# Walking the 512 columns of the feed-forward products in another order, layer by layer

## The chip, the cores and the metric

The kernel runs on one core of one Trainium2 chip, in one launch. The time is the device time of an execution in microseconds (us). The kernel before has a median of 2347.55 us over three runs (2344.4 to 2348.18).

## What is computed

Two blocks of a transformer work on 512 tokens of 1024 features in float32, with conditioning vectors that scale, shift and gate every layer. Of the six layers four are feed-forward layers, and the change touches these alone:

```python
def swiglu(y, w_gate, w_up, w_down):          # block 1, layers 1 and 3; hidden width 2816
    return (jax.nn.silu(y @ w_gate) * (y @ w_up)) @ w_down
...
y = jnp.square(jax.nn.relu(h @ mlp_w1[i])) @ mlp_w2[i]    # block 2, both MLPs; hidden width 4096
```

The others are a mixer of an mLSTM and a gated recurrence, gated linear attention, and differential attention. Their projections use the same two product helpers as the feed-forward layers.

## The kernel before

Every float32 value that goes into a large product is cut into two parts of type fp32r, a rounded high part and the rest (`parts2`, lines 320 to 328, for weights; line 606 for hidden values). A product of 128 rows of the contraction is then three matmuls into the same PSUM columns: high by high, high by low, low by high. Each matmul loads a stationary operand of 128 x 128 (LDWEIGHTS) and streams a moving operand (`rhs`) of up to 512 columns, one PSUM bank of 512 float32 per partition being the result.

Two helpers issue these matmuls. `fm` (lines 359 to 372) makes a feature-major product: the stationary operand is 128 columns of a weight, the moving one the tokens of the layer's input `X`, either all 512 (`FULL`) or a half of 256 (`HALVES`). `tm` (lines 374 to 388) makes a token-major product: the stationary operand is 128 tokens, the moving one 512 columns of a weight unit. In both, the moving operand and the result `p` are slices whose columns lie next to each other in memory.

`ffn` (lines 580 to 645) runs a layer in parts of its hidden width, `parts` tiles of 128 at a time. For every tile `hidden` calls `fm` (twice where there is a gate and an up weight), and ScalarE and VectorE turn the two PSUM results into the two parts of the hidden value, which lie in the buffers XB or XA. Then for two halves of the output columns and four blocks of 128 tokens `tm` multiplies the part by the down weight, and ScalarE or VectorE adds the result to `y` or to the residual. In the layers after the first, the first tiles (`nsplit`: 3 in the second feed-forward layer, 6 in the MLPs) run by halves of 256 tokens, so that they can start on the first half of the input. In the last layer `last_half` (lines 522 to 547) makes the last part, and its last token block has two products of 256 columns (lines 526 to 533).

PSUM banks are handed out in turn by role (`FFN_BANKS`, line 47: six for products, two for transposes). The program is one order of instructions per engine with semaphores between them; SyncE issues the loads of raw weights, ScalarE writes the high parts and VectorE the low parts, ahead of the products that use them. Conditioning vectors of later layers are computed meanwhile on VectorE and GpSimd at a pace set by `work` (lines 280 to 285).

The four layers start at lines 745, 1212, 1378 and 1613.

Of the kernel before, what the change touches and what calls it, by code (L numbers as in the profile page):

```python
# [35 lines left out]
def kernel(ctx: ExitStack, tc: tile.TileContext, a: dict, out: bass.AP):  # L36
    nc = tc.nc
    V, S, G, PE = nc.vector, nc.scalar, nc.gpsimd, nc.tensor
# [71 lines left out]
    def act(out, in_, func, **kw):  # L110
        """an activation; those of one table stay together, in the order of the program"""
# [12 lines left out]
    # two regions that hold plain values and rounded ones in turn, as tensors over the same bytes  # L124
# [93 lines left out]
    h = const.tile([128, 4, D], F32, tag="h", name="h")  # L218
# [7 lines left out]
    def ada_steps(w, c0, sc, bias, name, post=None, f=1.0):  # L226
        """one conditioning vector in eight steps: as columns, or (bias a row) as a row on every partition, times f
        times the row post"""
# [51 lines left out]
    def work(us):  # L280
        """conditioning vectors keep pace with the products"""
        clk[0] += us
        while jobs and clk[1] + clk[2] <= clk[0]:
            clk[1] += clk[2]
            bg()
# [44 lines left out]
    def group(w, k0, kn, c0, cn, uc=128):  # L330
        """[kn*128 rows, cn columns] of w as units of uc columns, each [128, 2, kn, uc]"""
# [9 lines left out]
    def group_k(w, k0, kn, c0, cn, uk):  # L341
        """the same cut into units of uk row tiles, each [128, 2, uk, cn]"""
# [14 lines left out]
    products, due = [], [0]  # L357

    def fm(p, wt, X, span, c=0):
        """feature-major product: 128 columns of a unit against the tokens of span"""  # L360
# [3 lines left out]
        for k in range(kn):  # L364
            xh, xl = X[k]
            wh, wl = wt[:, 0, k, c:c + 128], wt[:, 1, k, c:c + 128]
            PE.matmul(p, lhsT=wh, rhs=xh[:, s:s + n], start=k == 0, stop=False)  # L367
            PE.matmul(p, lhsT=wh, rhs=xl[:, s:s + n], start=False, stop=False)  # L368
            done = PE.matmul(p, lhsT=wl, rhs=xh[:, s:s + n], start=False, stop=k == kn - 1)  # L369
# [4 lines left out]
    def tm(p, wts, X, blk, c=0):  # L374
        """token-major product: 128 tokens against the columns of the units"""
# [5 lines left out]
        for wt in wts:  # L381
            for k in range(wt.shape[2]):
                xh, xl = X[n]
                PE.matmul(p, lhsT=xh[:, s:s + 128], rhs=wt[:, 0, k, cs], start=n == 0, stop=False)  # L384
                PE.matmul(p, lhsT=xh[:, s:s + 128], rhs=wt[:, 1, k, cs], start=False, stop=False)  # L385
                done = PE.matmul(p, lhsT=xl[:, s:s + 128], rhs=wt[:, 0, k, cs], start=False, stop=n == last)  # L386
# [6 lines left out]
    class Parts(list):  # L393
        """the two parts of a layer's input, by rows of features, and the tensors that hold them"""
# [22 lines left out]
    class Sums:  # L417
        """sums of squares of two token blocks by halves of the columns, and from them 1 / rms"""
# [18 lines left out]
    def scaled_to(dst, blk, r):  # L437
        """dst = the block of h times r"""
# [7 lines left out]
    def to_X(X, y, A, sh, half, role="pt"):  # L446
        """two token blocks of y to feature-major, modulated, in parts"""
# [25 lines left out]
    class PostEnd:  # L473
        """h += row * y / rms(y), then the next layer's input"""
# [25 lines left out]
    class GateEnd:  # L500
        """h += row * y, then the next layer's input; y in two parts, the first of them to early()"""
# [20 lines left out]
    def last_half(w, k0, X, y, row, gain):  # L522
        """h += row * y, then the last normalisation and out, by token blocks and parts of their columns"""
# [27 lines left out]
    def flush(ns=()):  # L551
        """the transposes of late, in parts behind the last ns of the products"""
# [94 lines left out]
    def tm_full(w, X, c0, sink):  # L647
        """token-major product with 512 columns"""
# [8 lines left out]
    # ======== start ========  # L657
# [1002 lines left out]
```

## Time and profile before

| | us |
|---|---|
| median of three runs | 2347.55 |
| lowest and highest | 2344.4, 2348.18 |
| span of the profiled execution | 2346.7 |
| PE busy in it | 2296.0 |
| VectorE busy | 1415.6 |
| ScalarE busy | 924.5 |
| GpSimd busy | 189.9 |

The profile states no time of its own for the profiled execution beside its span, from the first to the last instruction; the median of the runs lies 0.85 us above it. The page has the busy time of each engine (PE is TensorE's matmul, PEld its weight load, which overlaps), the span in 40 slices of 58.7 us, and the chain of work that ended last. Matmuls are pipelined: the duration of one includes its fill and drain, so that two matmuls overlap in the rows, and what a matmul costs in a stream is the distance from its start to the next one's.

### The profile page before, as it was taken

Reading aid. Unit: us, or ns where it says so; the run is one execution under the profiler, and the core shown is the slowest. Engines: PE = TensorE matmul, PEld = TensorE weight load, DVE = VectorE, ACT = ScalarE, POOL = GpSimd, SP = SyncE. Lnnn points to the kernel's source line nnn. Section 1 sums busy time; section 2 is a strip of 40 time slices with the busy share of each in tenths; the row PEclk is TensorE's granted clock in tenths of the full one; section 3 lists DMA queues with packets and bytes.
Section 4 is the critical chain, followed back from the end, with each engine's and each line's share of the span. In section 5 each row is a group of like instructions: output and inputs, shape, how many; then the busy total and the mean of one; then the engine's idle time right before and its main releaser. Section 6 shows DMA issues by size and latency. Waiting matters only on the chain.

```text
span 2346.7 us, 27950 instructions
## 1 busy us (share of the span) xinstructions
PE 2296.0 (98%) x10920; PEld 1849.9 (79%) x10920; DVE 1415.6 (60%) x2371; ACT 924.5 (39%) x1722; POOL 189.9 (8%) x126
## 2 busy tenths in 40 slices
PE   6999999999999999999999999999999999999998
PEld 4788887888678888888877887888776767888887
DVE  7846455765858645455654775567755577634364
ACT  4332224643656332224644443222345456323222
POOL 0111111000001101010000011011000010100000
PEclk9999999999999999999999999999999999999999
DMA  9755444445212655451432264445341312423221
GB/s 269 233 174 176 145 162 72 109 108 101 71 54 74 214 165 176 127 164 61 130 123 90 72 197 153 140 142 167 120 129 55 113 63 70 138 90 101 88 91 62
DMA packets 211733, 292.60 MB, mean 125 GB/s; under 512 B 7121, under 2 KB 120192, under 8 KB 211600
## 3 DMA queue, kind: packets, MB, share of 16 engines
q1 hardware_dynamic: 210960, 289.74, 40.7%
q8 instruction: 86, 1.41, 0.2%
q10 hardware_dynamic: 640, 1.07, 0.1%
q14 instruction: 47, 0.39, 0.1%
HBM read 288.68 MB, written 2.10 MB: 124 GB/s over the span
## 4 chain that ended last, share of the span: by engine, by line
PE 87%; DVE 5%; ACT 3%; DMA 2%; issue 2%; POOL 1%; POOLq 0%; SPq 0%; ACTq 0%; DVEq 0%
PE PS L386 13%; PE PS L367 13%; PE PS L384 13%; PE PS L368 13%; PE PS L385 13%; PE PS L369 13%; PE PS L1466 1%; DMA araw<-in_ada_w_dram 1%; ACT RS L118 1%; DVE w L328 1%; PE PS L901 1%; POOL sm L407 1%; PE PS L1495 1%; ACT tmp L118 1%; ACT w L118 1%
## 5 line engine op out<-in xcount | busy, mean ns | idle before, releaser
L328 DVE TENSOR_TENSOR w<-raw,w 128x1024 fp32r<-128x1024 f32 (+1 forms) x392 | 472.3, 1210 | 431.1 <-ACT w L118 430.4
L118 ACT ACTIVATE w<-raw 128x1024 fp32r<-128x1024 f32 (+1 forms) x392 | 389.2, 1000 | 519.7 <-PE PS L386 292.2
L368 PE MATMUL PS<-XAr,w 128*128 128x512 f32 (+1 forms) x1328 | 492.7, 371 | 1.1 <-DVE XAr L466 0.6
L369 PE MATMUL PS<-XAr,w 128*128 128x512 f32 (+1 forms) x1328 | 491.3, 370 | 0.0
L367 PE MATMUL PS<-XAr,w 128*128 128x512 f32 (+1 forms) x1328 | 489.7, 372 | 0.1
L384 PE MATMUL PS<-w,XAr 128*128 128x512 f32 x806 | 322.1, 400 | 1.0 <-DVE XAr L465 0.8
L385 PE MATMUL PS<-w,XAr 128*128 128x512 f32 x806 | 319.4, 397 | 0.0
L386 PE MATMUL PS<-w,XAr 128*128 128x512 f32 x806 | 319.1, 397 | 0.0
L368 PEld LDWEIGHTS PS<-XAr,w 128*128 128x128 f32 x1328 | 251.5, 189 | 48.1 <-DVE XAr L690 1.1
L367 PEld LDWEIGHTS PS<-XAr,w 128*128 128x128 f32 x1328 | 250.3, 189 | 48.9 <-issue 1.6
L369 PEld LDWEIGHTS PS<-XAr,w 128*128 128x128 f32 x1328 | 251.2, 189 | 45.2
L386 PE MATMUL PS<-w,XBr 128*128 128x512 f32 x704 | 279.8, 398 | 2.4 <-DVE XBr L606 2.0
L385 PE MATMUL PS<-w,XBr 128*128 128x512 f32 x704 | 280.2, 398 | 0.0
L384 PE MATMUL PS<-w,XBr 128*128 128x512 f32 x704 | 279.1, 397 | 0.1
L118 ACT ACTIVATE tmp<-PS 128x512 f32<-128x512 f32 (+3 forms) x227 | 104.4, 465 | 429.2 <-PE PS L369 339.5
L245 DVE SCALAR_TENSOR_TENSOR acc<-araw,silu_c,acc 128x512 f32<-128x512 f32 x266 | 199.3, 749 | 69.3 <-DMA araw<-in_ada_w_dram 65.0
L253 POOL PARTITION_ALL_REDUCE tmp<-acc x38 | 132.5, 3486 | 1068.4 <-DVE acc L245 700.0
L384 PEld LDWEIGHTS PS<-w,XAr 128*128 128x128 f32 x806 | 151.9, 188 | 37.7 <-ACT tmp L118 1.6
L385 PEld LDWEIGHTS PS<-w,XAr 128*128 128x128 f32 x806 | 152.0, 189 | 36.1 <-issue 1.6
L386 PEld LDWEIGHTS PS<-w,XAr 128*128 128x128 f32 x806 | 151.9, 189 | 36.1 <-issue 0.8
L386 PEld LDWEIGHTS PS<-w,XBr 128*128 128x128 f32 x704 | 132.3, 188 | 34.4 <-DVE XBr L606 2.8
L384 PEld LDWEIGHTS PS<-w,XBr 128*128 128x128 f32 x704 | 132.3, 188 | 33.4 <-ACT RS L118 0.5
(297 smaller groups left out, 2508.4 us busy)
## 6 DMA issues: line engine op xcount, KB each, us to landing
araw<-in_ada_w_dram SPq DMA_DIRECT2D x152, 512.0 KB
raw<-in_mlp_w_dram SPq DMA_DIRECT2D x56, 1024.0 KB
raw<-in_ffn_w_gate_dram SPq DMA_DIRECT2D x20, 1024.0 KB
raw<-in_ffn_w_up_dram SPq DMA_DIRECT2D x20, 1024.0 KB
raw<-in_ffn_w_down_dram SPq DMA_DIRECT2D x20, 1024.0 KB
raw<-in_w_in_dram SPq DMA_DIRECT2D x16, 1024.0 KB
raw<-in_gla_w_in_dram SPq DMA_DIRECT2D x12, 1024.0 KB
raw<-in_diff_w_in_dram SPq DMA_DIRECT2D x12, 1024.0 KB
```

The lines of the kernel that those rows point to most:

```text
L118: ins = S.activation(out, in_, func, **kw)
L245: V.scalar_tensor_tensor(acc, raw[:, k, :], col, acc, op0=ALU.mult, op1=ALU.add)
L253: G.partition_all_reduce(red, acc, channels=128, reduce_op=bass_isa.ReduceOp.add)
L328: V.tensor_tensor(wt[:, 1, ks], src[:, ks], wt[:, 0, ks].bitcast(F32), op=ALU.subtract)
L367: PE.matmul(p, lhsT=wh, rhs=xh[:, s:s + n], start=k == 0, stop=False)
L368: PE.matmul(p, lhsT=wh, rhs=xl[:, s:s + n], start=False, stop=False)
L369: done = PE.matmul(p, lhsT=wl, rhs=xh[:, s:s + n], start=False, stop=k == kn - 1)
L384: PE.matmul(p, lhsT=xh[:, s:s + 128], rhs=wt[:, 0, k, cs], start=n == 0, stop=False)
L385: PE.matmul(p, lhsT=xh[:, s:s + 128], rhs=wt[:, 1, k, cs], start=False, stop=False)
L386: done = PE.matmul(p, lhsT=xl[:, s:s + 128], rhs=wt[:, 0, k, cs], start=False, stop=n == last)
L407: G.tensor_tensor(r, ms, mhalf[:, 0:w], op=ALU.pow)
L901: PE.matmul(p[:, c * 128:(c + 1) * 128], lhsT=L[:, c * 128:(c + 1) * 128], rhs=R[:, c * 128:(c + 1) * 128], start=True, stop=True)
```

## The change

`fm` and `tm` send the moving operand and the result of each matmul through a new helper, `walked`. Where a walk is set and the operand has 512 columns, it views them as `a` blocks of `b` runs of `c` columns and reads or writes them run by run: the first run of each block, then the second run of each block, and so on. Both operands are walked alike, so that every value lands where it did before. The stationary operand is as it was, and so are the matmuls, their number and their order. A variable, `walk`, is set ahead of each feed-forward layer and cleared after it; operands of 256 columns are left as they were.

| layer | a, c | runs of a matmul | from one run to the next |
|---|---|---|---|
| feed-forward 1 | 2, 2 | 256 of 2 columns | 256 columns on, or back |
| feed-forward 2 | 4, 16 | 32 of 16 columns | 128 columns on, or back |
| MLP 1 | 2, 8 | 64 of 8 columns | 256 columns on, or back |
| MLP 2 | 2, 64 | 8 of 64 columns | 256 columns on, or back |

```diff
+    walk = [None]
+
+    def walked(ap):
+
+        if walk[0] is None or ap.shape[1] != 512:
+            return ap
+        a_, c_ = walk[0]
+        return ap.rearrange("p (a b c) -> p b a c", a=a_, c=c_)
...
     def fm(p, wt, X, span, c=0):
...
-            PE.matmul(p, lhsT=wh, rhs=xh[:, s:s + n], start=k == 0, stop=False)
-            PE.matmul(p, lhsT=wh, rhs=xl[:, s:s + n], start=False, stop=False)
-            done = PE.matmul(p, lhsT=wl, rhs=xh[:, s:s + n], start=False, stop=k == kn - 1)
+            xh, xl = walked(xh[:, s:s + n]), walked(xl[:, s:s + n])
+            PE.matmul(walked(p), lhsT=wh, rhs=xh, start=k == 0, stop=False)
+            PE.matmul(walked(p), lhsT=wh, rhs=xl, start=False, stop=False)
+            done = PE.matmul(walked(p), lhsT=wl, rhs=xh, start=False, stop=k == kn - 1)
...
     def tm(p, wts, X, blk, c=0):
...
-                PE.matmul(p, lhsT=xh[:, s:s + 128], rhs=wt[:, 0, k, cs], start=n == 0, stop=False)
-                PE.matmul(p, lhsT=xh[:, s:s + 128], rhs=wt[:, 1, k, cs], start=False, stop=False)
-                done = PE.matmul(p, lhsT=xl[:, s:s + 128], rhs=wt[:, 0, k, cs], start=False, stop=n == last)
+                wh, wl, p_ = walked(wt[:, 0, k, cs]), walked(wt[:, 1, k, cs]), walked(p)
+                PE.matmul(p_, lhsT=xh[:, s:s + 128], rhs=wh, start=n == 0, stop=False)
+                PE.matmul(p_, lhsT=xh[:, s:s + 128], rhs=wl, start=False, stop=False)
+                done = PE.matmul(p_, lhsT=xl[:, s:s + 128], rhs=wh, start=False, stop=n == last)
...
+    walk[0] = 2, 2
     Xm = new_X("xa")
     ffn(X, a["ffn1_w_gate"][0], ...
+    walk[0] = None
...
+    walk[0] = 4, 16
     X3 = new_X("xa")
     ffn(X2, a["ffn2_w_gate"][0], ...
+    walk[0] = None
...
+    walk[0] = 2, 8
     X5 = new_X("xa")
     ffn(X4, a["mlp_w1_2"][0], None, ...
+    walk[0] = None
...
+    walk[0] = 2, 64
     ffn(X6, a["mlp_w1_2"][1], None, ...
```

The rest of the diff takes out comments and docstrings.

## Rows read from the trace of the kernel before

**Rows 1.** The page: busy time of each engine; the span in 40 slices.
```profile
PE 2296.0 (98%) x10920; PEld 1849.9 (79%) x10920; DVE 1415.6 (60%) x2371; ACT 924.5 (39%) x1722; POOL 189.9 (8%) x126
...
PE   6999999999999999999999999999999999999998
...
PEclk9999999999999999999999999999999999999999
```

**Rows 2.** The page: the chain that ended last, by engine and by line.
```profile
PE 87%; DVE 5%; ACT 3%; DMA 2%; issue 2%; POOL 1%; POOLq 0%; SPq 0%; ACTq 0%; DVEq 0%
PE PS L386 13%; PE PS L367 13%; PE PS L384 13%; PE PS L368 13%; PE PS L385 13%; PE PS L369 13%; PE PS L1466 1%; DMA araw<-in_ada_w_dram 1%; ACT RS L118 1%; DVE w L328 1%; PE PS L901 1%; POOL sm L407 1%; PE PS L1495 1%; ACT tmp L118 1%; ACT w L118 1%
```

**Rows 3.** Windows of the four feed-forward layers; the header names the columns.
```profile
core 0: us, PE busy (x) PEld busy (x) DVE busy (x) ACT busy (x) POOL busy (x), PEclk, DMA share, GB/s
55.00:410.00 355.00, 354.39 (x1526) 283.81 (x1526) 209.40 (x304) 111.49 (x158) 47.17 (x40) 1.00 0.55 162
770.00:1112.00 342.00, 341.42 (x1475) 274.25 (x1474) 189.29 (x247) 101.66 (x145) 32.99 (x13) 1.00 0.46 149
1377.00:1705.00 328.00, 326.02 (x1402) 261.48 (x1401) 214.00 (x286) 100.78 (x142) 34.42 (x10) 1.00 0.48 154
2015.00:2346.00 331.00, 324.63 (x1411) 261.95 (x1409) 153.38 (x194) 96.67 (x137) 6.27 (x5) 0.99 0.30 95
```

**Rows 4.** Timeline of PE, matmuls of `fm`: start us, duration us, line.
```profile
770.24 0.40 PE L367 MATMUL PS<-XAr,w 128*128 128x512 f32 x1
770.47 0.39 PE L368 MATMUL PS<-XAr,w 128*128 128x512 f32 x1
...
781.95 0.40 PE L369 MATMUL PS<-XAr,w 128*128 128x512 f32 x1
```

**Rows 5.** Timeline of PE, matmuls of `tm` in the first layer.
```profile
399.52 0.39 PE L384 MATMUL PS<-w,XBr 128*128 128x512 f32 x1
...
402.55 0.40 PE L385 MATMUL PS<-w,XBr 128*128 128x512 f32 x1
```

**Rows 6.** Timeline of PE, matmuls of 256 columns in the mixer.
```profile
429.53 0.28 PE L369 MATMUL PS<-XAr,w 128*128 128x256 f32 x1
...
430.59 0.28 PE L369 MATMUL PS<-XAr,w 128*128 128x256 f32 x1
```

**Rows 7.** Timeline of PE, products of plain float32, 256 columns, in block 2.
```profile
1171.03 0.60 PE L1312 MATMUL PS<-XBf,RS 128*128 128x256 f32 x2
1171.46 0.59 PE L1317 MATMUL PS<-XBf,tmp 128*128 128x256 f32 x2
1171.89 1.03 PE L1312 MATMUL PS<-XBf,RS 128*128 128x256 f32 x4
1172.75 0.59 PE L1314 MATMUL PS<-st,XBf 128*128 128x256 f32 x2
```

**Rows 8.** Lines 925 and 606 on VectorE (durations ns min/median/max).
```profile
L925 DVE TENSOR_TENSOR tmp<-XBf x24: 415/418/428, 441.7 to 599.6; 128x256 f32<-128x256 f32 x24
L606 DVE TENSOR_TENSOR XBr<-tmp,XBr x85: 412/684/2732, 65.9 to 1675.1; 128x512 fp32r<-128x512 f32 x67, 128x256 fp32r<-128x256 f32 x18
```

**Rows 9.** Groups of PE by line and shape in 55 to 410 us: count, busy us, mean ns, idle before.
```profile
L368 PE MATMUL PS<-XAr,w 128*128 128x512 f32 x325 | 128.8, 397 | 0.0
...
L386 PE MATMUL PS<-w,XBr 128*128 128x512 f32 x176 | 69.9, 397 | 0.0
```

More of the change, by code (lines that the diff above doesn't have):

```diff
@@ L393 @@
     class Parts(list):
+        pass
     def new_X(bank="xa"):
```

## The prediction

> **What bounds the kernel now.** I read the page first: PE is busy 2296.0 of 2346.7 us, 9 tenths or more in every slice but the first and the last, at full granted clock, while VectorE has 60% and ScalarE 39% [rows 1]. Busy time of a pipelined engine could still hide waits, so the chain comes next: PE has 87% of it, and the six lines of `fm` and `tm` 13% each, 78% together [rows 2]. Then the four layers that the change touches, as windows: in 55 to 410 us PE is busy 354.39 of 355.00 us, in the others 341.42 of 342, 326.02 of 328 and 324.63 of 331, at a granted clock of 1.00, 1.00, 1.00 and 0.99 [rows 3]. The groups of that first window show no idle time ahead of the product lines [rows 9]. So in these layers nothing is waited for; a matmul starts when the one before has streamed. What one costs is the distance between starts, not its duration (397 ns on average, which overlaps the next): from 770.24 to 781.95 us there are 50 steps of `fm`, 234.2 ns each [rows 4], and from 399.52 to 402.55 us 13 steps of `tm`, 233.1 ns each [rows 5].
>
> Is that time the stream's, or a fixed cost of a matmul (its weight load, its dispatch)? Matmuls of 256 columns are 9 steps in 1.06 us apart, 117.8 ns [rows 6]: half of the columns, half of the time. So the time is proportional to the columns, 0.457 ns each, and the stream itself is the bound. [...] Plain float32 products stream at 1.72 us for 8 matmuls of 256 columns, 215 ns each, 0.84 ns a column [rows 7].
>
> **What the change does to this.** It adds no instruction, no wait, no transfer, and moves none: the count of matmuls and weight loads, the semaphores, the loads of SyncE and the work of the other engines are the same, and since both views of a bank and of an operand reach from its first to its last column, what has to wait for what is the same too. The only thing that can change is the time of a column in the stream of a walked matmul. How many are walked follows from the code (512 columns, walk set):
>
> - feed-forward 1, runs of 2: 22 tiles x 2 weights x 8 rows x 3 = 1056 in `fm`, 22 x 2 x 4 x 3 = 528 in `tm`: 1584 (the first window has three lines of `fm` with some 325 and three of `tm` with 176 [rows 9]; the rest of `fm` lies before 55 us, between waits for the first data)
> - feed-forward 2, runs of 16: 19 x 2 x 8 x 3 = 912, and 528: 1440
> - MLP 1, runs of 8: 26 x 8 x 3 = 624, and 32 x 2 x 4 x 3 = 768: 1392
> - MLP 2, runs of 64: 1392 less 18 that have 256 columns: 1374
>
> In all 5790, at 234 ns some 1355 us, 58% of the span. There is no cover: PE has no idle time in these layers, so every ns on a matmul of the first layer is 1.58 us of the end, and on all 5790 it is 5.79 us.
>
> What a hop between runs costs the stream, the trace of before does not show: every matmul in it reads and writes neighbouring columns. [...] Above: the slowest stream that the trace has on this engine, 0.84 ns a column [rows 7], 430 ns a matmul, +196 ns; or, if a run of two costs as much to fetch as four neighbouring columns do now, 2 x 234 = 468 ns, +234.
>
> The nearest row for a hop is on another engine: line 925 reads and writes 256 columns in runs of 1, 2, 4, 8, 16 and 32 with as many left out between, and takes 415 to 428 ns over all 24; the fastest 256 columns of line 606, side by side, take 412 [rows 8]. That is at most 16 ns over 256 columns and no trend to six sizes of run. VectorE is slower per column than PE, so this bounds nothing for a stream of 0.457 ns; but it says that operands of this memory are read and written in short runs at the same rate. I take zero for the hop in all four layers: in three of them (16, 8 and 64 columns) a run is long against anything that could be fetched at once, and for runs of 2 zero is the row that is nearest in kind.
>
> [...]
>
> **The sum.** 5790 x 0 ns: span 2346.7 as it was, median 2347.5. The median of the runs lies 0.85 us above the span, and I carry that over.
>
> **The rivals.**
>
> First, runs of 2 stream at half rate, and only these. [...] Place: feed-forward 1, both `fm` and `tm`. Price: 1584 x 0.196 = +310 us by the plain stream's rate, 1584 x 0.234 = +371 by double cost; 2658 to 2719, and 2718 for a full doubling. The point from which it decides is the length of run below which a fetch is wasted: if it is 4 (or 8), one layer pays, if it is 2, none.
>
> [...]
>
> Second, every hop costs something, whatever the run: p ns for each of 256, 32, 64 and 8 runs. [...] Against: line 925 makes up to 256 hops and takes at most 16 ns more for them [rows 8], 0.06 ns a hop. Worked out at p = 0.4 (between zero and 196/256 = 0.77): 1584 x 102 + 1440 x 12.8 + 1392 x 25.6 + 1374 x 3.2 ns = 162 + 18 + 36 + 4 = +220 us, 2568; at 0.77 it is some +424, 2771.
>
> Third, any walk puts the stream at the plain rate: 5790 x 0.196 = +1135 us, 3482. [...]
>
> [...]
>
> Fifth, the change doesn't reach the chip, since the view is put back into plain order on the way: then the time is the forecast's, and only the rows of PE, or an experiment with another order, could tell it from a free hop.
>
> **How the numbers follow.** No cost at any run: 0.53, with the fifth rival's 0.03 at the same time. First rival 0.25, second 0.07, third 0.04, fourth 0.08. A measurement of this kernel can tell about 0.2%, 5 us, from no change: the runs of before lie within 3.8 us. The forecast's own range is 2341 to 2354. It holds only 0.56, so the range has to reach to the first rival, whose bounds are 2658 and 2719, and takes in the second's middle on the way: 2341 to 2722, some 0.86 with the part of the second that lies below. The fourth, the third and the upper end of the second are left out, 0.14. Faster by over 0.2%: the fourth and a little scatter, 0.09. Within 0.2%: 0.54. Slower: the first three and a little scatter, 0.37.
>
> **What would show it.** In the profile after, the distance between starts of the walked matmuls in each layer: 234 in all four by the forecast; 430 to 470 in the first layer and 234 elsewhere by the first rival; about 336, 247, 260 and 237 by the second at its middle; 430 everywhere by the third; under 230 by the fourth. The mixers, which are not walked, must stay at 234 in every case, and each layer's window as long as 512-column matmuls make it. The forecast is wrong if the first layer's window grows beyond 355 us, or if the layers differ by run length. It would also be wrong, with the right hop, if PE began to wait in a layer, which the idle times before its lines would show.

## The result and the profile after

The changed kernel takes 2506.43 us (median of four runs, 2504.86 to 2508.23) against 2347.86 us for the kernel before on the same footing (2344.4 to 2348.34): 1.0685 times as long, 95% interval 1.0672 to 1.0698. The forecast was 2347.5, no change. The profiled execution has a span of 2503.1 us, 156.4 more than before.

The page of the kernel after: busy time of each engine, PE and its granted clock in 40 slices, and the chain that ended last, by engine and by line.

```profile
PE 2454.6 (98%) x10920; PEld 1862.0 (74%) x10920; DVE 1412.7 (56%) x2371; ACT 926.0 (37%) x1722; POOL 187.8 (8%) x126
...
PE   6999999999999999999999999999999999999998
...
PEclk9999999999999999999999999999999999999999
...
PE 89%; DVE 4%; ACT 3%; issue 1%; DMA 1%; POOL 1%; POOLq 0%; ACTq 0%; DVEq 0%
PE PS L377 14%; PE PS L376 14%; PE PS L378 14%; PE PS L396 13%; PE PS L394 13%; PE PS L395 13%; PE PS L1482 1%; ACT RS L118 1%; PE PS L913 1%; DMA araw<-in_ada_w_dram 1%; POOL sm L417 1%; PE PS L1511 1%; DVE w L328 1%; ACT tmp L118 1%; ACT w L118 0%
```

Against [rows 1, 2] the counts of instructions are the same, the busy time of VectorE, ScalarE and GpSimd is the same to 3 us, the granted clock is the same. PE is busy longer, by 158.6 us, and it has 89% of the chain, where it had 87%; its weight loads, which overlap, are 12.1 us longer. `fm` is now at lines 376 to 378 and `tm` at 394 to 396. Span less busy time of PE is 48.5 us, and it was 50.7. So no wait was added: something that PE does takes longer.

Windows of the four feed-forward layers, columns as in [rows 3], each over nearly the same matmuls as there (the count stands in brackets behind PE's busy time).

```profile
55.00:560.40 505.40, 505.40 (x1550) 298.44 (x1549) 210.67 (x315) 113.72 (x160) 45.49 (x40) 1.00 0.38 113
920.00:1257.20 337.20, 336.55 (x1474) 274.18 (x1473) 189.65 (x247) 101.94 (x145) 33.01 (x13) 1.00 0.47 151
1522.00:1861.00 339.00, 338.33 (x1403) 263.24 (x1402) 213.82 (x286) 100.80 (x142) 33.70 (x10) 1.00 0.47 150
2171.00:2502.60 331.60, 325.08 (x1414) 262.40 (x1413) 153.78 (x195) 96.69 (x137) 6.28 (x5) 0.99 0.30 95
```

For the same matmuls (to three) the second layer takes 337.2 us instead of 342, the third 339 instead of 328, the fourth 331.6 instead of 331. The first has 1550 in 505.4 us where 1526 took 355. PE has under 0.7 us of idle time in the first three and 6.5 in the last, where it had 6.4.

The timeline of PE tells what one matmul costs: start us, duration us, line. In order: four matmuls in a row in the first part of the first layer; two that are 30 steps apart in its second part; the first walked matmul of layer 2; two 30 steps apart in that layer; two in MLP 1; two in MLP 2.

```profile
98.71 0.50 PE L376 MATMUL PS<-XAr,w 128*128 128x512 f32 x1
99.04 0.52 PE L377 MATMUL PS<-XAr,w 128*128 128x512 f32 x1
99.39 0.50 PE L378 MATMUL PS<-XAr,w 128*128 128x512 f32 x1
99.72 0.50 PE L376 MATMUL PS<-XAr,w 128*128 128x512 f32 x1
...
248.67 0.50 PE L376 MATMUL PS<-XAr,w 128*128 128x512 f32 x1
...
258.47 0.50 PE L376 MATMUL PS<-XAr,w 128*128 128x512 f32 x1
...
920.23 0.40 PE L376 MATMUL PS<-XAr,w 128*128 128x512 f32 x1
...
929.67 0.39 PE L378 MATMUL PS<-XAr,w 128*128 128x512 f32 x1
...
936.57 0.39 PE L378 MATMUL PS<-XAr,w 128*128 128x512 f32 x1
...
1579.80 0.41 PE L376 MATMUL PS<-XAr,w 128*128 128x512 f32 x1
...
1587.10 0.41 PE L376 MATMUL PS<-XAr,w 128*128 128x512 f32 x1
...
2229.61 0.39 PE L377 MATMUL PS<-XBr,w 128*128 128x512 f32 x1
...
2236.59 0.39 PE L377 MATMUL PS<-XBr,w 128*128 128x512 f32 x1
```

In the first layer three matmuls take 1.01 us, some 336 ns each (line 377 0.35, the other two 0.33); in its second part 30 steps take 9.80 us, 327 ns each. In layer 2 30 steps take 6.90 us, 230 ns; in MLP 1 7.30, 243 ns; in MLP 2 6.98, 233 ns. The first walked matmul of layer 2 starts at 920.23, where it started at 770.24 [rows 4]: all that lies ahead of it is the first layer and a mixer that is not walked, and it lost 150.0 us. With layer 2 at -4.8, MLP 1 at +11.0 and MLP 2 at nothing that is 156.2 of the 156.4 us of the span.

So the place is that of the first rival, runs of 2 in the first layer, and the size is not: 150 us over 1584 matmuls are 95 ns each, where it asked for 196 to 234.

### The profile page after: what moved, and what is told of

Its sections match the earlier page's. It is cut to its first block, busy times and chain, and to the rows that moved or that the text cites. A ratio compares the mean times of both kernels' runs of the same rounds, so it can differ in the third digit from the quotient of the medians.

```text
span 2503.1 us, 27960 instructions
## 1 busy us (share of the span) xinstructions
PE 2454.6 (98%) x10920; PEld 1862.0 (74%) x10920; DVE 1412.7 (56%) x2371; ACT 926.0 (37%) x1722; POOL 187.8 (8%) x126
## 4 chain that ended last, share of the span: by engine, by line
PE 89%; DVE 4%; ACT 3%; issue 1%; DMA 1%; POOL 1%; POOLq 0%; ACTq 0%; DVEq 0%
PE PS L377 14%; PE PS L376 14%; PE PS L378 14%; PE PS L396 13%; PE PS L394 13%; PE PS L395 13%; PE PS L1482 1%; ACT RS L118 1%; PE PS L913 1%; DMA araw<-in_ada_w_dram 1%; POOL sm L417 1%; PE PS L1511 1%; DVE w L328 1%; ACT tmp L118 1%; ACT w L118 0%
## 5 line engine op out<-in xcount | busy, mean ns | idle before, releaser
L377 PE MATMUL PS<-XAr,w 128*128 128x512 f32 (+1 forms) x1328 | 532.5, 401 | 1.1 <-DVE XAr L476 0.6
L378 PE MATMUL PS<-XAr,w 128*128 128x512 f32 (+1 forms) x1328 | 527.5, 398 | 0.0
L376 PE MATMUL PS<-XAr,w 128*128 128x512 f32 (+1 forms) x1328 | 526.1, 400 | 0.7 <-DVE XAr L475 0.7
L376 PEld LDWEIGHTS PS<-XAr,w 128*128 128x128 f32 x1328 | 253.8, 192 | 82.3 <-issue 34.1
L377 PEld LDWEIGHTS PS<-XAr,w 128*128 128x128 f32 x1328 | 253.8, 191 | 78.0 <-issue 1.5
L378 PEld LDWEIGHTS PS<-XAr,w 128*128 128x128 f32 x1328 | 253.5, 191 | 76.0 <-issue 1.1
L396 PE MATMUL PS<-w,XBr 128*128 128x512 f32 x704 | 299.6, 426 | 1.2 <-DVE XBr L616 0.7
L394 PE MATMUL PS<-w,XBr 128*128 128x512 f32 x704 | 300.0, 427 | 0.1
L395 PE MATMUL PS<-w,XBr 128*128 128x512 f32 x704 | 300.0, 426 | 0.0
```

The costliest lines, as they stand in the source:

```text
L376: PE.matmul(walked(p), lhsT=wh, rhs=xh, start=k == 0, stop=False)
L377: PE.matmul(walked(p), lhsT=wh, rhs=xl, start=False, stop=False)
L378: done = PE.matmul(walked(p), lhsT=wl, rhs=xh, start=False, stop=k == kn - 1)
L394: PE.matmul(p_, lhsT=xh[:, s:s + 128], rhs=wh, start=n == 0, stop=False)
L395: PE.matmul(p_, lhsT=xh[:, s:s + 128], rhs=wl, start=False, stop=False)
L396: done = PE.matmul(p_, lhsT=xl[:, s:s + 128], rhs=wh, start=False, stop=n == last)
```

## The experiments

The runs are called e1 to e12 in this order. In all of them the distance between starts of matmuls of 512 columns is read in each stretch, as above; before, it is 234 everywhere (233 in `tm`). A time without a count of runs is that of a single run; the argument there goes by the distances within its trace, where the mixers' `tm`, which is not walked, stays at 233 to 234 wherever PE doesn't wait. (a, c) is a walk in the diff's own form: a blocks, runs of c columns. Where a kernel uses several orders, each holds for one part of a feed-forward layer's hidden width, `fm` and `tm` of that part.

**Which of the two operands pays?** Two kernels, edited from the kernel after in `fm` (shown) and in `tm` alike: the walk in the moving operand alone (first diff), and in the result alone (second).

```diff
-            PE.matmul(walked(p), lhsT=wh, rhs=xh, start=k == 0, stop=False)
+            PE.matmul(p, lhsT=wh, rhs=xh, start=k == 0, stop=False)
```
```diff
-            xh, xl = walked(xh[:, s:s + n]), walked(xl[:, s:s + n])
+            xh, xl = xh[:, s:s + n], xl[:, s:s + n]
```

> Only the moving operand is walked, the result is written in plain order (so the columns of the feed-forward products land permuted). In the changed kernel a matmul started 327 to 335 ns after the one before with runs of 2, 230 to 232 with runs of 16, 243 with runs of 8, 233 with runs of 64, against 234 before. Theory M (the hops cost in fetching the moving operand): the same four distances here, time about 2506 us. Theory R (they cost in adding into the result): 234 in all four layers, about 2348 us. If both sides have a part, the first layer lies between 240 and 320.

> Only the result is walked, the moving operand is read in plain order (so the columns land permuted). Theory M: 234 ns in all four layers, about 2348 us. Theory R: 327 to 335, 230 to 232, 243 and 233 ns as in the changed kernel, about 2506 us.

Moving operand alone: 2503.23 us, and in every layer the distances of the kernel after to a nanosecond (in the first part of the first layer 335.5 ns over 33 steps, and 335.7 there). Result alone: 2345.17 us, beside 2347.61 for the kernel before on that chip. Its timeline in the first layer, where each bank is written in 256 runs of two:

```profile
69.75 0.40 PE L377 MATMUL PS<-XAr,w 128*128 128x512 f32 x1
...
76.78 0.39 PE L377 MATMUL PS<-XAr,w 128*128 128x512 f32 x1
```

These are 30 steps in 7.03 us, 234 ns. The whole price, and also the small gain of layer 2 and the small loss of MLP 1, is the reading of the moving operand. Writing PSUM in runs of 2, 16, 8 or 64 columns costs nothing that shows beside a stream of 234 ns (the kernel with all four layers written so: 2345.17 us). Runs of one column in PSUM were not tried.

**Is it the first layer alone?** The walk is taken out there and left in the other three.

```diff
-    walk[0] = 2, 2
+    walk[0] = None
     Xm = new_X("xa")
```

> The walk of the first layer (runs of 2) is taken out, the three others stay. If the layers are independent and the distances of the changed kernel hold, the first layer returns to 234 ns a matmul; what stays against before is about 912 x -4.2 + 528 x -1.8 ns in the second layer (-4.8 us), 1392 x +9.2 ns in the first MLP (+12.8 us) and 0 in the last: 2347.9 + 8 = 2356 us, ratio 1.0034. If the first layer's loss was only a part of a common one, it lies above 2370.

2352.72 us (eight runs), 1.0029 times the kernel before (1.0017 to 1.004): +5 us for three layers, where the windows say -4.8 and +11.0, some 6. All else, over 150 us, was runs of two.

**A price per hop, or a length of run?** The next kernel has many forms, both operands walked as in the change.

```diff
-    walk[0] = 2, 2
+    plan[:] = [(2, 4), (2, 16), (2, 32)]
...
-    walk[0] = 4, 16
+    plan[:] = [(2, 128), (4, 2), (8, 2)]
...
-    walk[0] = 2, 8
+    plan[:] = [(4, 8), (8, 8), (16, 8), (32, 8), (64, 8)]
...
-    walk[0] = 2, 64
+    plan[:] = [(4, 16), (8, 16), (16, 16), (4, 64), (32, 16)]
```

> Sixteen walks (blocks a, run c), one for each part of each layer: first layer (2,4) (2,16) (2,32), second (2,128) (4,2) (8,2), first MLP (4,8) (8,8) (16,8) (32,8) (64,8), last (4,16) (8,16) (16,16) (4,64) (32,16). Theory H (each hop costs the same, 0.37 ns as 95 ns over 256 hops): (2,4) +47 ns over 234, runs of 8 +24, of 16 +12, of 32 +6, of 128 +1, of 2 +95 whatever the blocks. Theory L (runs of 2 waste half of what a fetch brings, longer runs nothing): only (4,2) and (8,2) stand out, at 327 or more, and (2,4) is at 234. Theory D (the distance between blocks decides, 128 columns being good and 256 bad): runs of 8 over 4 blocks at about 230, over 2 at 243; runs of 16 over 2 blocks above 234.

2603.93 us. (4, 8), (16, 8) and (32, 8) take 230 to 234, (8, 8) 240 in `fm` and 247 in `tm`, (4, 16) 230, (8, 16) and (16, 16) 233 to 240. With two blocks, runs of 4 take 247 (`fm`) and 253 (`tm`), of 16 240, of 32 233 and 236, of 128 234. But runs of two with four blocks:

```profile
899.73 0.64 PE L378 MATMUL PS<-XAr,w 128*128 128x512 f32 x1
...
908.63 0.64 PE L377 MATMUL PS<-XAr,w 128*128 128x512 f32 x1
```

20 steps in 8.90 us are 445 ns, and with eight blocks it is 490. The number of hops is 256 in (2, 2), (4, 2) and (8, 2) alike, and the price is +95, +211 and +256. So it isn't a price per hop. The number of columns in a run does not set it either: what is different between (2, 2) and (4, 2) is how soon the walk comes back to where it was, after 2 columns elsewhere or after 6. Theory H falls with that. L is right that (4, 2) and (8, 2) alone stand far out, but (2, 4) is not at 234, and L has no reason for the step from (2, 2) to (4, 2). D had its three numbers, runs of 8 over 4 blocks at 230, over 2 at 243, and of 16 over 2 above 234; it says nothing of runs of two, and e6 tests it further.

**Pieces of four.** The theory for the next kernel: if four neighbouring columns count as one piece, what matters is how its columns are visited. Moving operand alone:

```diff
+        'pairs_far': ('p (q r c) -> p r q c', {'r': 2, 'c': 2}),    0 1 4 5 8 9 ..., then 2 3 6 7 ...
+        'swap_in4': ('p (q r c) -> p q c r', {'r': 2, 'c': 2}),     0 2 1 3 4 6 5 7 ...
+        'evens': ('p (q r) -> p r q', {'r': 2}),                    0 2 4 6 ..., then 1 3 5 7 ...
+        'step4': ('p (q r) -> p r q', {'r': 4}),                    0 4 8 ..., then 1 5 9 ...
+        'fours_far': ('p (q r c) -> p r q c', {'r': 2, 'c': 4}),    0 1 2 3 8 9 10 11 ...
+        'eights_far': ('p (q r c) -> p r q c', {'r': 2, 'c': 8}),
```

> Only the moving operand is walked (columns land permuted; the result is not the reference's). One order for each part: first layer: the first pair of every four, then the second pairs (P); inside every four the order 0 2 1 3 (S); even columns, then odd ones (E). Second layer: every fourth column, four times (F4); the first four of every eight, then the second fours (Q); the same with eights (O). First MLP, parts 2 to 5: P, Q, (2,2), (2,4). Last MLP, parts 2 to 5, as (blocks, run): (64,2), (32,2), (64,4), (32,4). Products of 256 columns at the start of a layer: (2,2) with blocks 128 columns apart, (4,2) 64 apart, (2,8) 128 apart. Theory G (the operand is fetched in pieces of four columns; a run that leaves half of a piece unused pays for it unless the rest is asked for within the next run or two): P, E, (64,2), (32,2) about 450 to 490 ns; F4 near 900; S, Q, O, the fours at 230 to 250; 256 columns: (2,2) about 165, (4,2) about 240, (2,8) 117 to 122. Theory A (each column or run that doesn't follow the one before costs a step, wherever it lies): S and E are the worst, with 511 steps, above 400; P like (2,2), 327; the fours 280. Theory T (the distance between successive runs decides: 256 columns mild, 128 or less bad): 256-column (2,2) like (4,2) of 512, about 222; P, with a distance of 4 columns, tells least and may be anything; Q and O differ from 234.

2965.91 us. The first pair of every four, then the second pairs: 453 to 459. The same columns swapped within a piece: 234. Evens then odds 453, every fourth column 460, fours of every eight 232, eights 230 to 233. The timeline, first the pairs, then the swap:

```profile
89.42 0.63 PE L396 MATMUL PS<-XAr,w 128*128 128x512 f32 x1
...
98.58 0.63 PE L395 MATMUL PS<-XAr,w 128*128 128x512 f32 x1
...
299.69 0.40 PE L395 MATMUL PS<-XAr,w 128*128 128x512 f32 x1
...
306.73 0.39 PE L395 MATMUL PS<-XAr,w 128*128 128x512 f32 x1
```

20 steps are 458 ns each, 30 are 235. So a run of two that is left for good does stream at about half rate (453 to 459 ns where the plain order takes 234), as the first rival had it; order within four neighbouring columns is free (234 to 235 for the swap). Runs of two with 32 and 64 blocks belong with the pairs: (32, 2) takes 432, (64, 2) 460. But a theory in which each fetch of a piece serves its columns one after the other wanted some 900 ns for every fourth column, and that took 460, no more than pairs. Half right. Theory A falls with the swap, which has 511 steps and takes 234. Theory T, that 256 columns is a mild distance and 128 a bad one, falls with the products of 256 columns: two blocks in runs of 2, here 128 columns apart, take 165 to 167 ns where the plain ones take 118, in proportion what (2, 2) costs at 512; (4, 2) takes 225, (2, 8) 123.

**More sizes and blocks**, both operands walked.

```diff
+    plan[:] = ['4_8', '32_8', '4_4']
+    plan[:] = ['16_4', '8_4', 'r4c4']
+    plan[:] = ['4_32', '4_16', '4_32', '32_4', 'r4c8']
+    plan[:] = ['4_8', '4_16', '4_32', '32_8', '4_8']
```

> Both operands walked, as in the changed kernel, looking for orders that are faster than neighbouring columns. (blocks, run) by part: first layer (4,8) (32,8) (4,4); second (16,4) (8,4) and, of every sixteen columns, the first fours, then the second and so on; first MLP (4,32) (4,16) (4,32) (32,4) and the same with eights of every 32; last MLP (4,8) (4,16) (4,32) (32,8) (4,8). From what was measured, (4,8), (4,16) and (32,8) should lie at 230 to 232 ns against 234; theory G (pieces of four columns) says that runs of 4 lose nothing by themselves, so that all lie within 228 to 250. Theory D (blocks 128 columns apart are good, 256 bad): (4,4) and (4,32) are at 230 as well. If the gain of (4,16) belonged to its layer and not to its order, (4,16) in the MLPs is at 234.

2382.58 us. In runs of 4: 247 to 253 with 2 blocks (above), 266 with 4, 278 with 8, 246 with 16, 226 with 32. In runs of 8 with 4 and 32 blocks 230 to 233; of 16 with 4 blocks 230 to 232, in the MLPs too, so that gain belongs to the order and not to its layer; of 32 with 4 blocks 233 to 240. Theory D falls with (4, 4) and (4, 32), and G's bound of 250 with (4, 4) and (8, 4). So beside the large effect there is a small one, within -8 and +44 ns in these runs, that changes with the blocks and so with the distance of the hop, and one form beats the plain order by more than 4 ns: (32, 4).

**(32, 4) in the four feed-forward layers (first diff, one layer of four), and in every product (second).**

```diff
-    walk[0] = 2, 2
+    walk[0] = 32, 4
```
```diff
-        if walk[0] is None or ap.shape[1] != 512:
+        if ap.shape[1] not in (256, 512):
             return ap
-        a_, c_ = walk[0]
-        return ap.rearrange("p (a b c) -> p b a c", a=a_, c=c_)
+        return ap.rearrange("p (a b c) -> p b a c", b=4, c=4)
```

> The same places as the changed kernel, but one order in all four layers: (32,4), runs of 4 columns, 16 columns from one to the next (first the first four of every sixteen columns, then the second, and so on). The looks at orders gave 225 to 227 ns a matmul for it against 234 to 233. If it holds in all layers: 5790 x 7.5 ns = 43 us less, 2304 us, ratio 0.981. If the products then wait for weights or hidden values, less: above 2325. If the gain belonged to the layers that were looked at, 2335 or more.

> The same order in every product of 512 columns, the mixers' too (2352 more matmuls), and in those of 256 columns (1284), with 16 columns from run to run. If the mixers' products stream at 226 as well and their time is on the path: 2352 x 7.5 + 1284 x 3.5 ns = 22 us less than with the feed-forward layers alone, 2282 us. In the mixers PE waits for other engines here and there, so from 2282 to 2304.

The first takes 2308.63 us, 0.9841 times the kernel before (0.9824 to 0.9857), with distances of 226 in `fm` and 220 to 230 in `tm`. The first was foretold (2304). The second takes 2309.47, 0.9843 (0.9828 to 0.9857): the mixers' `tm` fell to 225 (231 in part of the second) and the 256 columns to 115, and the time stayed. That was a miss: a shorter stream in the mixers did not move the end. PE only came earlier to what it waits for: its waits for VectorE's `Y`, ahead of the transposes to the next layer's input, are 14.1 us in all, and 5.8 in the run without the mixers.

**Which order is faster than the plain one?** Moving operand alone; first 508 columns from column 0, 2, 1 and 3 on, then two, four and eight pieces in turn, column by column.

```diff
+        'R2': ('p (q r c) -> p q c r', {'r': 2, 'c': 4}),           0 4 1 5 2 6 3 7 8 12 ...
+        'R4': ('p (q r c) -> p q c r', {'r': 4, 'c': 4}),           0 4 8 12 1 5 9 13 ...
+        'R8': ('p (q r c) -> p q c r', {'r': 8, 'c': 4}),
+        'A2': ('p (a b) -> p b a', {'a': 2}),                       0 256 1 257 2 258 ...
+        'A4': ('p (a b) -> p b a', {'a': 4}),                       0 128 256 384 1 129 ...
+        'step8': ('p (q r) -> p r q', {'r': 8}),
```

> Only the moving operand is walked (columns land permuted, and where 508 columns are read the last four are left out; the result is not the reference's; PSUM is set to zero once at the start, some 4 us). By part: first layer: 508 neighbouring columns from column 0, from 2, from 1. Second: 0 4 1 5 2 6 3 7 in every eight (R2); 0 4 8 12 1 5 9 13 and so on in every sixteen (R4); the same over eight fours (R8). First MLP, parts 2 to 5: columns of two halves in turn (A2), of four quarters in turn (A4), (2,2), 508 columns from column 3. Last MLP, parts 2 to 5: every 8th column, every 16th, every 32nd, then (32,4). Theory F (columns are taken four at a time: four in one aligned piece cost 1.83 ns, four that aren't cost 3.5 to 3.8, however many pieces they touch, and half of that saving comes back when the same two pieces are wanted by the next four): R2, A2 and (2,2) 327 to 350; R4, A4 and R8 about 450; every 8th, 16th and 32nd about 460; 508 columns from 1, 2 or 3 either 327 to 450 (each four straddles two pieces) or 232 (the piece is still there). Theory P (each new piece costs 1.8 ns and a few are kept): R4 and A4 at 234 to 260 if four are kept; every 8th to 32nd 900. Theory B (pieces lie in banks by their address, and it is a clash that costs): every 16th faster than every 8th, as (32,4) is faster than (16,4).

2712.88 us. Where a product starts matters little: 233, 235, 230 and 227 ns in `fm` for 508 columns, 227 to 233 in `tm`. The orders in turn, on the timeline: R2, then R4, then every eighth column.

```profile
779.68 0.38 PE L402 MATMUL PS<-XAr,w 128*128 128x512 f32 x1
...
786.15 0.38 PE L402 MATMUL PS<-XAr,w 128*128 128x512 f32 x1
...
879.70 0.43 PE L401 MATMUL PS<-XAr,w 128*128 128x512 f32 x1
...
887.76 0.43 PE L401 MATMUL PS<-XAr,w 128*128 128x512 f32 x1
...
2249.55 0.61 PE L401 MATMUL PS<-XBr,w 128*128 128x512 f32 x1
...
2258.19 0.61 PE L403 MATMUL PS<-XBr,w 128*128 128x512 f32 x1
```

Two pieces in turn take 6.47 us for 30 steps, 215.7 ns, 18 less than in the plain order. It is the same with the pieces 4 columns or 256 columns apart (A2, 215.8), though no two columns that follow each other in the stream lie together. Four in turn take 269 (R4) to 276 (A4), eight 480, every eighth column 432, every 16th and 32nd 433 to 437. None of the theories, as they were stated, fits all of these: F had R2 and A2 at 327 to 350, P the steps at 900, and B every 16th column faster than every 8th.

**Odd and even places of the stream.** One way of sorting the orders fits all the large steps so far: look at the columns in even places of the stream by themselves, and at those in odd places by themselves, and count how many of a piece of four neighbours come there before the next piece. In the plain order the even places hold 0, 2, then 4, 6: two columns of each piece (234 ns). In R2 and A2 they hold 0 1 2 3: four (215.8). In pairs, evens, steps, (4, 2), (8, 2), (32, 2) and (64, 2) they hold one of a piece and go elsewhere (432 to 490). In (2, 2) they hold 0, 256, 2, 258: one of a piece, and it comes back next but one (327 to 347). The next expectation calls the even and the odd places lanes. That the engine fetches by them side by side is its theory; what the traces show is orders and their times. The next kernel has orders on which this rule and its rivals differ.

```diff
+        'T2': ('p (r c s) -> p s c r', {'r': 2, 's': 2}),           0 256 2 258 4 260 ..., then the odd ones
+        'T4': ('p (r c s) -> p s c r', {'r': 2, 's': 4}),           0 256 4 260 ...
+        'A8': ('p (a b) -> p b a', {'a': 8}),
+        'R2c8': ('p (q r c) -> p q c r', {'r': 2, 'c': 8}),         0 8 1 9 2 10 ...
+        'R4c2': ('p (q r c) -> p q c r', {'r': 4, 'c': 2}),         0 2 4 6 1 3 5 7 ...
```

> Only the moving operand is walked (columns land permuted; the result is not the reference's). New theory L (two lanes): the odd and the even columns of the stream are fetched side by side, and each lane runs at full rate while at least two of its columns in a row lie in one piece of four neighbours; a lane that changes its piece at every column takes twice as long; one that changes between two pieces and comes back lies between. It fits the orders so far. Orders that tell it from theory N (what counts is that neighbours come close together in the stream): from two halves in turn, the even columns of both, then the odd ones (0 256 2 258 4 260 ...; T2): L 230 to 235 ns (each lane has two columns in a piece), N and theory G (half of each piece is wasted in a pass) 430 to 460, as for even, then odd columns of one row (E, again here). The same with every fourth column (T4): L 430 to 460. Columns of eight blocks in turn (A8): L 430 to 480 (each lane goes round four pieces). 0 8 1 9 2 10 and so on in every sixteen, and 0 16 1 17 in every 32: L 216, as for halves in turn (A2). 0 2 4 6 1 3 5 7 in every eight (R4c2): L 327 to 347 (each lane changes between two pieces, as with (2,2)), G 234 or less, since both pieces are read at once. By part: first layer T2, T4, A8; second: 0 8 1 9, R4c2, T2; first MLP, parts 2 to 5: T2, E, first pairs and then second pairs of every four, T4; last MLP, parts 2 to 5: T2, T4, R4c2, 0 16 1 17.

2919.38 us. The timeline for T2, then R4c2, then evens:

```profile
71.64 0.39 PE L390 MATMUL PS<-XAr,w 128*128 128x512 f32 x1
...
78.66 0.40 PE L390 MATMUL PS<-XAr,w 128*128 128x512 f32 x1
...
1129.51 0.51 PE L390 MATMUL PS<-XAr,w 128*128 128x512 f32 x1
...
1136.31 0.51 PE L389 MATMUL PS<-XAr,w 128*128 128x512 f32 x1
...
1799.58 0.64 PE L389 MATMUL PS<-XAr,w 128*128 128x512 f32 x1
...
1808.64 0.64 PE L388 MATMUL PS<-XAr,w 128*128 128x512 f32 x1
```

234 (30 steps), 340 and 453 ns (20 each). T2 and evens read the same columns in steps of two; by place in the stream, the even places hold two of each piece in the one and one in the other. Theories N and G had T2 at 430 to 460, and G had R4c2 at 234 or less. T4 (453) and the pieces 8 and 16 columns apart (216) came as the rule has them; A8 took 487 to 489 where it had 430 to 480. The rule, with what each order showed:

| what the even places take of a piece, and the odd ones alike | orders | ns |
|---|---|---|
| four of a piece, then the next | R2, A2, R2 with pieces 8 and 16 apart | 215.8 |
| two of a piece, then the next | plain, swap, T2, runs of 8 or more | 230 to 248 |
| two, by hops in runs of 4 | (2, 4) to (64, 4) | 220 to 278 |
| four of each of two pieces, visited in turn | R4, A4 | 269 to 276 |
| two of each of two pieces, visited in turn | (2, 2), R4c2 | 327 to 347 |
| one, or four pieces in turn | evens, pairs, steps, T4, (4, 2), (8, 2), (32, 2), (64, 2), R8, A8 | 431 to 490 |

Counted over the stream as a whole the rule fails: the pairs of e5 take two neighbours of each piece one after the other, and 458 ns. Counted by places, the large steps of the table agree with it; the differences within a row of the table do not follow from it. The theory of lanes foretold these orders; what in the engine makes the order count, lanes or something else, no trace shows.

**A kernel that uses it.** Four of a piece in the even places, and four in the odd ones, can be had without a walk of the result: the operand is stored evens first, odds behind, and read from the two halves in turn. The stream is then in plain order. The conversion of the weights and of the layers' inputs does the turning.

```diff
-    def parts2(wt, src):
+    def alt(ap):
+        return ap.rearrange("p m (a b) -> p m a b", a=2)
+    def evens(ap):
+        return ap.rearrange("p m (b a) -> p m a b", a=2)
+    def stream(ap, s, n):
+        return ap.rearrange("p (a b) -> p b a", a=2)[:, s // 2:(s + n) // 2, :]
+    def parts2(wt, src, turned=False):
...
+                act(alt(wt[:, 0, ks]), evens(src[:, ks]), AF.Copy)
...
+                V.tensor_tensor(alt(wt[:, 1, ks]), evens(src[:, ks]), alt(wt[:, 0, ks].bitcast(F32)), op=ALU.subtract)
...
+            xh, xl = (stream(x, s, n) if X.turned else x[:, s:s + n] for x in (xh, xl))
...
+                wh, wl = (stream(wt[:, i, k, :], c, p.shape[1]) for i in range(2))
```

> The kernel before, with another change: no result is walked; instead the inputs of the feed-forward layers and all weights of token-major products are stored with their even columns first and their odd ones behind (ScalarE and VectorE read every second column of what they convert), and the matmuls read the two halves in turn, so that the results come out in plain order. The looks gave 216 ns for that order. If it holds: feed-forward 5790 x 18 = 104 us less, their 1284 products of 256 columns 9 ns each, 12 us, and up to 1920 matmuls of the mixers 17 ns each, 33 us at most: 2200 to 2232 us, ratio 0.937 to 0.951. If the conversions slow down so far that PE waits for weights: between that and 2348. If reading two halves in turn is fast only with the columns in the old places: 2340 or more.

2247.14 us (five runs), 0.9577 times the kernel before (0.9564 to 0.9591): 99 us faster than before and 259 faster than the changed kernel. Its page, its timeline in the first layer, and its groups of weight conversions on VectorE, turned and plain:

```profile
PE 2165.1 (96%) x10920; PEld 1852.7 (83%) x10920; DVE 1457.2 (65%) x2371; ACT 996.8 (44%) x1722; POOL 195.1 (9%) x126
...
PE 79%; DVE 9%; ACT 5%; DMA 4%; issue 2%; POOL 1%; SPq 0%; POOLq 0%; ACTq 0%; DVEq 0%
```
```profile
79.64 0.38 PE L391 MATMUL PS<-XAr,w 128*128 128x512 f32 x1
...
86.12 0.38 PE L391 MATMUL PS<-XAr,w 128*128 128x512 f32 x1
```
```profile
L341 DVE TENSOR_TENSOR w<-raw,w 128x1024 fp32r<-128x1024 f32 x188 | 278.4, 1491 | 194.5 <-ACT w L118 194.0
L349 DVE TENSOR_TENSOR w<-raw,w 128x1024 fp32r<-128x1024 f32 x152 | 203.5, 1344 | 166.4 <-ACT w L118 165.1
```

216 ns a step, as foretold, and 15 us short of the range of times. PE's share of the chain fell from 87% [rows 2] to 79%, VectorE's rose from 5% to 9%: with a shorter stream the conversions and the hidden values come late at more places, and PE waits 5.7 us for hidden values and 3.8 for turned weights, where it waited 2.0 for the one and no wait is listed for the other. The turned subtraction takes 1491 ns, the plain one of the same shape beside it 1344; in the kernel before that shape takes 1291, and the 1210 in the next expectation is a mean over two shapes.

The last run leaves the mixers' weights plain.

```diff
-                parts2(wt, raw[:, u:u + m, :], True)
+                parts2(wt, raw[:, u:u + m, :], tw[0])
...
+        tw[0] = True        (at the start of ffn)
...
+        tw[0] = False       (at its end)
```

> The kernel before with the turned storage (even columns first, odd ones behind, the two halves read in turn) only where the inputs and weights of the four feed-forward layers are made; the mixers' weights stay plain. This asks what the mixers' part of the last experiment was worth. There the mixers' windows were 4, 6 and 3 us shorter than before, and their conversions on VectorE dearer (1491 ns each, 1210 before). If the mixers' faster token products pay more than the dearer conversions cost, this run is 10 to 15 us slower than that one: 2257 to 2262 us. If they are paid for by stalls elsewhere, it is as fast or faster: 2235 to 2250 us. In both theories the feed-forward products stand at 215.8 ns and the mixers' at 233 to 234 ns.

2259.29 us (four runs), 0.9624 (0.9608 to 0.964). So the mixers were worth 12 us, the first of the two theories, and the feed-forward layers 87. Windows of the first two mixers, columns as in [rows 3], in e11 and then in e12:

```profile
378.90:741.70 362.80, 343.68 (x2022) 291.37 (x2022) 251.79 (x518) 207.44 (x432) 26.66 (x22) 0.98 0.38 92
1052.10:1319.60 267.50, 259.36 (x1460) 224.84 (x1460) 175.64 (x289) 145.85 (x282) 19.32 (x14) 1.00 0.33 106
```
```profile
378.30:745.30 367.00, 353.74 (x2022) 291.71 (x2022) 249.69 (x516) 203.50 (x432) 26.78 (x22) 0.98 0.37 91
1056.00:1329.90 273.90, 268.54 (x1460) 224.55 (x1460) 173.58 (x289) 140.67 (x282) 19.34 (x14) 1.00 0.32 104
```

In the first mixer PE is busy 10.1 us less with the turned weights, and the window is 4.2 us shorter; the rest became idle time of PE. In the second it is 9.2 and 6.4.

But the range of e11 ended at 2232 us with nothing from the mixers; it missed by the feed-forward layers. They were to give 104 us by 5790 matmuls and 12 by 1284 of 256 columns, and e12 gave 87. Windows of the four layers in e12, to be set beside [rows 3]:

```profile
55.00:385.50 330.50, 327.64 (x1523) 283.98 (x1522) 218.54 (x301) 121.37 (x157) 50.20 (x40) 1.00 0.58 173
745.00:1063.00 318.00, 313.97 (x1459) 272.94 (x1458) 196.45 (x245) 110.31 (x144) 33.06 (x13) 1.00 0.50 161
1329.50:1643.00 313.50, 307.17 (x1416) 267.30 (x1415) 221.35 (x288) 116.83 (x145) 37.02 (x10) 0.99 0.51 162
1948.50:2257.00 308.50, 301.47 (x1414) 263.71 (x1412) 162.52 (x195) 110.39 (x137) 6.50 (x5) 0.99 0.31 103
```

PE is idle for 20.3 us of these windows and for 9.5 of those before, over nearly as many matmuls: about 11 of the missing 29 us are new waits. Some 6 more are missing since 384 of the 1284 are the mixers', which read plain columns, and the other 900 fell from 118 to 112 ns, by 6 or 7 and not 9. The rest was not taken apart.

## Why the prediction was wrong, point by point

**What bounds the kernel.** Right. The stream of PE was the bound, nothing covered it, and what a walked matmul cost went to the end: in the first layer the starts are 327 to 336 ns apart where they were 234, 93 to 102 more, and the first walked matmul of layer 2 came 150.0 us later, 95 for each of 1584. The counts by layer held too. With streams shorter than before (e8, e11, e12) PE began to wait, and less arrived.

**The range.** 2506.43 us lies inside the stated 2341 to 2722, but only because the range was drawn out to the first rival's prices. No sum of the prediction comes nearer than 2568, the second rival's, whose rule fell. That is luck.

**The step that failed** is the zero for the hop in runs of two. I took it from VectorE, "the row that is nearest in kind", though I had written that VectorE is slower per column than PE and "bounds nothing" for a stream of 0.457 ns [rows 8]. It was another engine; the kernel after has 327 to 336 ns where by that row it had to stay at 234, and e1 and e2 put all of it in the reading of PE's moving operand. The rows that bore on it were my own of PE: its time goes with the columns, 117.8 ns for 256 and 234 for 512 [rows 4, 6], so that what a column costs goes in full into the distance; e1, e9 and e11 show that the order of reading changes it, to 336 and to 215.8. No row before had a hop on PE, and for that the first rival should have weighed more than 0.25.

**The zero for the other three layers** was nearly right: -4 ns in runs of 16 (`fm`; under -2 in `tm`), +9 in runs of 8, 0 in runs of 64, together +5 us (e3). But that they are long "against anything that could be fetched at once" was no measurement: no run shows how much that is.

**The first rival** had the place (feed-forward 1, `fm` and `tm`), and its price was too high: +310 to +371 for what was +150. Where the other two columns of a piece are not asked for soon, as in pairs or (4, 2), the price is about its full doubling, 432 to 490 ns; in (2, 2), where they are asked for two runs later, it is 327 to 347. The rule of odd and even places sorts both, and R4c2 (340) with them. How many columns a fetch takes, from which the rival decides, no run shows.

**The second rival** at its middle named 336, 247, 260 and 237 ns, and 327 to 336, 230, 243 and 233 came, so its total was the nearest to the measured time. But that is the number p that I chose, not its rule: with the same 256 hops (4, 2) costs +211 and (8, 2) +256, and with 32 hops layer 2 is faster than none.

**The third rival** falls with e2 and MLP 2. **The fifth** falls with every row of the first layer.

**The fourth**, under 230 ns in the walked layers, didn't happen in this change: layer 2 comes down to 230 in `fm`, 4 ns below the plain order, and the others stay above that. That another order is faster than the plain one is right all the same: R2, A2 and e11 have 215.8 ns, and e12 shows -87 us in the feed-forward layers, with their products of 256 columns.

## What to carry to other kernels

Where PE streams without a gap, the order in which the moving operand is read has a price in ns per matmul (from -18 to +256 here, on 234), and it is read from the distance between starts of neighbouring matmuls, not from another engine's rows. With operands of this type a result may be written in runs (of two and more, as tried here: 234 ns in e2), but the moving operand should keep eight or more columns together (14 ns or less of 234), or come from two regions in turn (215.8). A few orders tried on the chip were worth 4% here (e11).

## What the runs showed of the hardware that was not expected

- The plain order is not the fastest. 512 neighbouring columns of fp32r take 234 ns; the same columns taken from two regions in turn take 215.8 (e9 to e12).
- Runs of two columns cost from +93 ns a matmul to +256. (2, 2), which comes back after two columns elsewhere, takes 327 to 347; those that come back later or never take some twice the plain time, in no order of the return: (32, 2) 432, (4, 2) 445, pairs 453 to 459, (64, 2) 460, (8, 2) 490. Orders of single columns stream at the plain rate (swap and T2, 234), at about half of it (evens and steps, 432 to 460) or faster (A2, 215.8).
- Two neighbouring columns of a piece, left for good, do not stream at the plain rate: 0 1 4 5 ... takes 453 to 459, 0 2 1 3 ... 234.
- A result that is written in runs of two takes 234 ns, as one in a row (e2).

Open is what sets the smaller differences: runs of four are at 220 to 230 ns with 32 blocks and at 278 with 8, runs of 16 with 4 blocks gain 4 and runs of 8 with 2 lose 9, and in the first layer `fm` has 331, 346 and 330 ns on its three lines in the first and third part and 327 on each in the second. The distance of the hop and the buffer differ between these; no run takes the two apart. Open is also what in the engine makes the order count: the rule of odd and even places foretold T2 and R4c2, against two other theories, but what is measured is the order of columns and its time.
